# Taking one of the 16 DMA engines out of one late store: 120 partitions and 8 in place of 128

## The chip, the core and the metric

The kernel runs on one core of a Trainium2 chip. Times are microseconds of device time; a time quoted for a kernel is the median of its runs. "Span" is the length of the one profiled execution, and positions in it are counted from its start.

SBUF and PSUM are the memories that the kernel's tiles are allocated in; a tile here has 128 partitions. A *packet* is one row of the trace's DMA table: a piece of a transfer, moved by one DMA engine. A *completion* is one increment of a transfer's semaphore by one DMA engine; the store of a group shows 16 of them in the kernel before. SP is the engine whose instructions issue the transfers.

## The reference

```python
# x: (8, 16, 256, 512) float32, weight: (8, 16, 512, 384) float32
def reference(x, weight):
    return np.matmul(x, weight).astype(np.float32)
```

128 independent products of 256x512 by 512x384. The kernel reads 168 MB and writes 50 MB.

## The kernel before

The kernel takes four products at a time as a "group", 32 groups in all. For each it loads 2 MB of x and twice 1.5 MB of weights, casts both to bf16, transposes x on TensorE, multiplies, copies PSUM to an output tile and stores it. All transfers are issued from one queue (SP). SP loads four groups ahead.

```python
    G = 4; R = G * M // P; T = R // 2; NG = B // G      # R = 8 rows a partition, T = 4, NG = 32
    XS, WS, OS = 2, 2 * G // D, 4                       # buffers of x, weights, output
    LAG = 4
    ...
    out_sb = sbuf("out_sb", [P, R, N], fp32, OS)        # 128 partitions of 8 x 384 x 4 = 12288 B
    ...
    def store(e, t, U, s, pieces=1):
        n = t * U + s
        dram = o_rows[bass.ds(n * (G * M), G * M)].rearrange("(p r) n -> p r n", r=R)
        for q in range(pieces):
            rows = slice(q * R // pieces, (q + 1) * R // pieces)
            e.wait_ge(o_copied, n * T + ((q + 1) * T // pieces + BIAS))
            e.dma_start(out=dram[:, rows], in_=out_sb[s % OS][:, rows]).then_inc(
                o_out[s % OS], 16
            )
    ...
    def on_sync(e):
        U = OS
        for n in range(LAG):
            load(e, 0, NG, n)
        rounds = (NG - LAG) // U
        with e.Fori(0, rounds) as t:
            for s in range(U):
                load(e, t, U, LAG + s)
                store(e, t, U, s)
        for n in range(rounds * U, NG):                 # groups 28 to 31: stores alone are left
            if n + LAG < NG:
                load(e, 0, NG, n + LAG)
            store(e, 0, NG, n, T if n == NG - 1 else 1) # the last group in four pieces
        for s in range(OS):
            e.wait_ge(o_out[s], 16 + 16 * (NG // OS + (T - 1 if s == (NG - 1) % OS else 0)))
```

Of the kernel before, what the change touches and what calls it, by code (L numbers as in the profile page):

```python
# [12 lines left out]
def kernel(  # L13
# [7 lines left out]
    P = 128  # L21

    b1, b2, M, K = x.shape
# [6 lines left out]
    o_rows = out.rearrange("b1 b2 m n -> (b1 b2 m) n")  # L30
# [9 lines left out]
    G = 4  # L40
    C = P // G
    R = G * M // P
    T = R // 2
# [3 lines left out]
    NG = B // G  # L47

    XS, WS, OS = 2, 2 * G // D, 4
    BS, TS, WBS = 1, 2, 2 * G  # L50
    PT, PO = 4, 2

    LAG = 4

    ctx.enter_context(tc.tile_critical(no_gpsimd_drain=True))  # L55

    def sbuf(name, shape, dtype, n):
        return [
            ctx.enter_context(nc.sbuf_tensor(f"{name}{s}", shape, dtype)) for s in range(n)
        ]  # L60
# [6 lines left out]
    def sems(name, n):  # L67
        return [tc.alloc_semaphore(f"{name}{s}") for s in range(n)]
# [9 lines left out]
    out_sb = sbuf("out_sb", [P, R, N], fp32, OS)  # L78
# [6 lines left out]
    id_done, x_cast, w_cast, t_made, t_copied, p_made, o_copied = (  # L85
        sems(name, 1)[0]
        for name in (
            "id_done", "x_cast", "w_cast", "t_made", "t_copied", "p_made", "o_copied"
        )
    )  # L90
    x_in, w_in, o_out = sems("x_in", XS), sems("w_in", WS), sems("o_out", OS)


    BIAS = 8


    def load(e, t, U, s):
        n = t * U + s
        if not isinstance(n, int) or n >= XS:
            e.wait_ge(x_cast, n + (1 - XS))  # L100
        e.dma_start(  # L101
            x_sb[s % XS][:],
            x_rows[bass.ds(n * (G * M), G * M)].rearrange("(p r) k -> p r k", r=R),
        ).then_inc(x_in[s % XS], 16)
        for d in range(G // D):
            slot = (s * (G // D) + d) % WS
            if not isinstance(n, int) or n >= 2:
                e.wait_ge(w_cast, n * (G * S) + ((d + 1) * D * S - 2 * G * S))  # L108
            e.dma_start(  # L109
                w_sb[slot][:],  # L110
                w_rows[bass.ds(n * (G * K) + d * (D * K), D * K)].rearrange(
                    "(p k) n -> p k n", k=S * KO
                ),
            ).then_inc(w_in[slot], 16)
# [6 lines that stand above are left out]
            e.wait_ge(o_copied, n * T + ((q + 1) * T // pieces + BIAS))  # L121
            e.dma_start(out=dram[:, rows], in_=out_sb[s % OS][:, rows]).then_inc(
                o_out[s % OS], 16
            )

    def cast_x(e, t, U, s):
# [80 lines left out]
# [9 lines that stand above are left out]
        for n in range(rounds * U, NG):  # L216
            if n + LAG < NG:
                load(e, 0, NG, n + LAG)
            store(e, 0, NG, n, T if n == NG - 1 else 1)
        for s in range(OS):  # L220
            e.wait_ge(o_out[s], 16 + 16 * (NG // OS + (T - 1 if s == (NG - 1) % OS else 0)))

    def on_vector(e):
        U = 2
# [34 lines left out]

    on_gpsimd(nc.gpsimd)  # L260
    on_sync(nc.sync)
    on_vector(nc.vector)
    on_tensor(nc.tensor)
# [31 lines left out]
```

## Time and profile before

| | before |
|---|---|
| time | 519.69 us (519.62 to 519.71) |
| span of the profiled run | 517.8 us |
| last copy of output ends | 510.80 us |
| last DMA packet ends | 515.97 us |
| last completion arrives | 516.38 us |
| DMA rate in the middle | about 430 GB/s |

The page's lines for this, and what is read from them, are in the prediction below. The trace also dates each packet (start, duration, bytes) and each increment of a semaphore, one for each engine that takes part in a transfer. It does not number the engines.

### The profile page before, as it was taken

The numbers are of one execution on the slowest core, as the hardware profiler recorded it, in microseconds if no ns is written. First come the engines' busy times: TensorE is split into PE (matmuls) and PEld (weight loads), VectorE is DVE, ScalarE is ACT, GpSimd is POOL, SyncE is SP. The second block draws the span as 40 slices with busy tenths as digits, with TensorE's granted clock in tenths as the row PEclk, the third lists the DMA queues.
The fourth block names the chain that finished last, engine by engine and source line by source line (L and its number), as shares of the span: only waits on it lengthen the run. The fifth ranks groups of instructions, "written<-read, shape, count | busy, mean of one in ns | idle before, by whom it ended". The sixth has DMA issues, their size and how long they took to land.

```text
span 517.8 us, 11229 instructions
## 1 busy us (share of the span) xinstructions
PE 314.3 (61%) x4608; PEld 198.2 (38%) x4608; DVE 323.9 (63%) x384; ACT 212.9 (41%) x193; POOL 0.7 (0%) x6
## 2 busy tenths in 40 slices
PE   0588674576655676555766557665566655676653
PEld 0455443343433443333434334343344333443432
DVE  0788867655577555775556765557755577555670
ACT  3156462454324553245533345523455233553332
POOL 0000000000000000000000000000000000000000
PEclk9988896787868886787878678866877686777867
DMA  8999999999999999999999999999999999999995
GB/s 332 433 423 428 425 431 429 429 431 424 428 431 430 428 427 429 429 429 430 431 424 431 429 433 426 426 431 427 432 429 428 427 430 428 432 430 426 428 430 233
DMA packets 18869, 218.18 MB, mean 421 GB/s; under 512 B 2096, under 2 KB 2096, under 8 KB 2608
## 3 DMA queue, kind: packets, MB, share of 16 engines
q1 hardware_dynamic: 18864, 218.11, 99.3%
q8 instruction: 3, 0.05, 0.0%
q14 instruction: 2, 0.02, 0.0%
HBM read 167.77 MB, written 50.33 MB: 421 GB/s over the span
## 4 chain that ended last, share of the span: by engine, by line
DMA 81%; DVE 13%; issue 2%; PE 2%; ACT 1%; SPq 0%; DVEq 0%; ACTq 0%
DMA w_sb<-in_weight_dram 81%; DVE w_bf L149 12%; PE po L182 2%; ACT x_bf L131 0%; DVE x_t L155 0%; SPq L109 0%; ACT out_sb L196 0%; SPq L101 0%; DVEq L144 0%; DVEq L226 0%; SPq L108 0%; ACTq L195 0%; SPq L290 0%; SPq L55 0%
## 5 line engine op out<-in xcount | busy, mean ns | idle before, releaser
L149 DVE CAST w_bf<-w_sb 64x1536 bf16<-64x1536 f32 x256 | 244.5, 955 | 179.1 <-DMA w_sb<-in_weight_dram 172.1
L182 PE MATMUL po<-w_bf,x_t 128*32 128x384 bf16 x4096 | 231.4, 400 | 121.4 <-DVE x_t L155 121.4
L196 ACT COPY out_sb<-po 128x768 f32<-128x768 f32 x128 | 99.4, 803 | 289.3 <-PE po L182 289.3
L182 PEld LDWEIGHTS po<-w_bf,x_t 128*32 128x32 bf16 x4096 | 124.8, 116 | 225.3 <-DVE x_t L155 131.1
L168 PE MATMUL pt<-identity,x_bf 128*128 128x128 f32 x512 | 82.8, 325 | 74.3 <-ACT x_bf L131 74.3
L131 ACT CAST x_bf<-x_sb 128x2048 bf16<-128x2048 f32 x64 | 118.5, 1901 | 7.3 <-DMA x_sb<-in_x_dram 7.3
L168 PEld LDWEIGHTS pt<-identity,x_bf 128*128 128x128 f32 x512 | 73.3, 213 | 86.1 <-issue 86.1
L155 DVE COPY x_t<-pt 128x1024 bf16<-128x1024 bf16 x128 | 79.4, 683 | 1.0
L131 ACT ACT_TABLE_LOAD x1 | 1.3, 1283 | 1.3 <-PEq L232 1.3
masks.py:199 POOL TENSOR_SCALAR_AFFINE_SELECT identity<-identity 128x128 f32<-128x128 f32 x1 | 0.3, 294 | 0.2 <-POOL identity L202 0.2
L202 POOL MEMSET identity<- 128x128 f32 x1 | 0.2, 205 | 0.5 <-SPq L55 0.5
L279 POOL MEMSET const-bfloat16-1.0<- 128x1 bf16 x1 | 0.1, 102 | 0.0
L279 POOL MEMSET const-uint8-127<- 128x1 uint8 x1 | 0.1, 102 | 0.0
L279 POOL MEMSET const-float32-0.0<- 128x1 f32 x1 | 0.1, 99 | 0.2 <-issue 0.2
L279 POOL MEMSET const-float32-1.0<- 128x1 f32 x1 | 0.1, 99 | 0.0
## 6 DMA issues: line engine op xcount, KB each, us to landing
w_sb<-in_weight_dram SPq DMA_DIRECT2D x64, 1536.0 KB, 27.5
x_sb<-in_x_dram SPq DMA_DIRECT2D x32, 2048.0 KB, 25.8
out_dram<-out_sb SPq DMA_DIRECT2D x31, 1536.0 KB, 30.6
out_dram<-out_sb SPq DMA_DIRECT2D x4, 384.0 KB, 4.0
```

The costliest lines, as they stand in the source:

```text
L131: ins = e.copy(out=x_bf[s % BS][:, :, h], in_=x_sb[s % XS][:].rearrange("p r (q s c) -> p r s q c", s=S, c=KO)[:, :, h],)
L149: e.tensor_copy(out=w_bf[(s * G + d * D + a) % WBS][h * HP : (h + 1) * HP], in_=w_sb[slot][a * HP : (a + 1) * HP, h * KO : (h + 1) * KO, : ...
L155: e.tensor_copy(out=x_t[s % TS][:, 2 * q : 2 * q + 2], in_=pt[(s * T + q) % PT][:].bitcast(bf16),).then_inc(t_copied, 1)
L168: ins = e.transpose(pt[(s * T + q) % PT][:, rr, h, :], words[:, 2 * q + rr, h :: KO // 2], identity[:],)
L182: ins = e.matmul(po[(s * T + q) % PO][mine, rr, :N], x_t[s % TS][:, 2 * q + rr, ko // 2, mine, ko % 2], w_bf[(s * G + i) % WBS][:, ko, :], ...
L196: e.copy(out=out_sb[s % OS][:, 2 * q : 2 * q + 2, :], in_=po[(s * T + q) % PO][:, :, :N],).then_inc(o_copied, 1)
L202: e.memset(identity[:], 0.0).then_inc(id_done, 1)
L279: nc = _bacc.Bacc("TRN2", target_bir_lowering=False, num_devices=1)
```

## The change

Its intent: one of the 16 DMA engines, meant to be the last, gets no part of the store of group 28, so that it has less queued ahead of the end. The store is cut into partitions 0 to 119 and partitions 120 to 127. The recorded texts call the engine that is to be left out engine 15; that is a name, since no trace numbers the engines.

```diff
+    SKIP, SKIPPING = 120, NG - OS
...
+    def store_skipping(e, n):
+
+        dram = o_rows[n * (G * M) : (n + 1) * (G * M)].rearrange("(p r) n -> p r n", r=R)
+        e.wait_ge(o_copied, n * T + T + BIAS)
+        for parts in (slice(0, SKIP), slice(SKIP, P)):
+            e.dma_start(out=dram[parts], in_=out_sb[n % OS][parts]).then_inc(
+                o_out[n % OS], 16
+            )
...
-            store(e, 0, NG, n, T if n == NG - 1 else 1)
+            if n == SKIPPING:
+                store_skipping(e, n)
+            else:
+                store(e, 0, NG, n, T if n == NG - 1 else 1)
         for s in range(OS):
-            e.wait_ge(o_out[s], 16 + 16 * (NG // OS + (T - 1 if s == (NG - 1) % OS else 0)))
+            more = {(NG - 1) % OS: T - 1, SKIPPING % OS: 1}.get(s, 0)
+            e.wait_ge(o_out[s], 16 + 16 * (NG // OS + more))
```

## The prediction

> **What bounds the kernel now.** I read the page from the top. Part 2 says which resource is full, part 4 says what the end waited for.
>
> ```profile
> DMA  8999999999999999999999999999999999999995
> GB/s 332 433 423 428 425 431 429 429 431 424 428 431 430 428 427 429 429 429 430 431 424 431 429 433 426 426 431 427 432 429 428 427 430 428 432 430 426 428 430 233
> ...
> q1 hardware_dynamic: 18864, 218.11, 99.3%
> ...
> DMA 81%; DVE 13%; issue 2%; PE 2%; ACT 1%; SPq 0%; DVEq 0%; ACTq 0%
> ```
>
> The 16 DMA engines are busy from the second slice to the last but one and move about 430 GB/s; no compute engine passes 63% of the span. So the transfers set the pace. The chain of part 4 agrees (81% of it is weight loads), but it follows instructions and stops at the last copy into the output buffer. In order of time its end is:
>
> ```profile
> 502.32 7.66 PE po L182 x66
> 510.00 0.80 ACT out_sb L196
> ```
>
> The last piece of output is thus ready at 510.80 us and the span ends at 517.8 us. Those 7 us belong to the stores. The timeline of the DMA queue shows when the last ones were issued, five groups of 1536 KB, the last in four pieces (eight issues):
>
> ```profile
> 470.50 40.66 SPq L122 DMA_DIRECT2D out_dram<-out_sb  x8
> ```
>
> The table of stretches and the DMA view of 512 to 517 us (40 slices of 0.125 us) show how they drain:
>
> ```profile
> 505.00:510.00 5.00, 4.95 (x100) 2.60 (x92) 0.00 (x0) 2.43 (x3) 0.00 (x0) 0.81 0.94 390
> 510.00:512.00 2.00, 0.00 (x0) 0.00 (x0) 0.00 (x0) 0.80 (x1) 0.00 (x0) 1.00 0.79 315
> 512.00:514.00 2.00, 0.00 (x0) 0.00 (x0) 0.00 (x0) 0.00 (x0) 0.00 (x0) 0.94 0.42 167
> 514.00:516.00 2.00, 0.00 (x0) 0.00 (x0) 0.00 (x0) 0.00 (x0) 0.00 (x0) 0.50 0.06 25
> ...
> DMA  9999932321000000000000000010000000000000
> GB/s 393 418 418 393 393 123 98 123 98 74 25 25 25 25 25 25 25 25 25 25 25 25 25 25 25 25 49 25 25 25 25 0 0 0 0 0 0 0 0 0
> ```
>
> Full rate until about 512.6, then 98 to 123 GB/s for half a microsecond, then 25 GB/s until 515.9. One packet of 3072 B in each slice of 0.125 us is 25 GB/s, and a sixteenth of 430 is 27: for the last 2.7 us **one DMA engine works alone**, and 0.06 of 16 engines is one.
>
> That it is one engine that fell behind can be followed in the completions. Every transfer raises its semaphore sixteen times, once for each engine, and the trace dates each. For the stores of some groups, in us, the median of the sixteen and the last one:
>
> ```
> group   median   last    behind
>  4      132.1    133.6     1.5
> 16      322.8    325.3     2.5
> 24      450.0    453.1     3.1
> 28      501.2    504.8     3.6
> 30      508.4    512.7     4.3
> ```
>
> Three others sit some 1.5 us behind all along; three 16 KB instruction fetches of about 1 us each at 6, 35 and 43 us fit that. One falls back steadily. The last group's pieces end, in packets, at about 512.6 us on twelve engines, at 513.2 to 513.3 on the three, and at 515.97 on the slow one; the completions arrive about 0.4 us later, the last at 516.38.
>
> [...] 128 partitions take 16 engines with 8 partitions each (the trace agrees: 8 packets of 12288 B for each completion)[...]. [...] the slow engine's store packets follow each other without a gap to the end. So work left out earlier in its queue moves all later work forward.
>
> **The change part by part.**
> - Removed from engine 15: 8 packets of 12288 B. A packet mostly took 460 to 475 ns, on the slow engine up to 535. Between the slow engine's completions of groups 27 and 28 lie 504.75 - 500.97 = 3.78 us, so about 3.8 us goes.
> - [...]
> - Added on SP: one more issue, 0.36 us, at about 471 us. SP then waits for group 29's copies, done near 481, so it is off the path.
> - Loads: all are issued before this store [...]. The weights land at the same time, the compute ends at the same 510.80 us.
>
> Now the end. If engine 15 is the slow one, its last packet would be at 515.97 - 3.8 = 512.2 us. But the last piece's data is issued after 510.80 us, and engines without backlog end it at about 512.6, so the slow engine joins those. The end passes to the three engines that are 1.5 us behind: last completion at 513.65. That is 516.38 - 513.65 = **2.73 us** earlier. [...] After the last completion, 1.4 us to the span's end stays. In time: 519.69 - 2.73 = 516.96, or 519.69 - 2.26 = 517.43. I cannot tell which from this trace[...], so I lean to 517.3.
>
> **The rivals.**
> - *The slow engine is not the fifteenth.* [...] For it: the trace has no engine numbers. Against it: the change singles out the last engine, and the 3.8 us that it takes away is nearly the amount by which one engine is behind when this store runs (3.6 us). I give this one in ten.
> - *The stores are hidden or the compute sets the end.* Then freeing an engine brings nothing below what compute allows. It speaks for this that the last issue is at 510.8 us and twelve engines end already at 513.0. It is a floor: at most 516.38 - 513.0 = 3.4 us can be had, 516.3.
> - *The 120-partition transfer is dealt out otherwise*, on fewer engines. If all the first part ran on 8 engines, each would carry 15 packets in place of 8 and the end would move out by about 3 us less what slack there is: 521 to 523. [...] Under one in twenty.
> - *The whole kernel speeds up by the slow engine's share.* No: nothing before 471 us changes, and the loads are already queued.
>
> **Range and chances.** The two branches give 516.96 and 517.43; the runs before lie within 0.1 us. A little less gain than worked out is possible if the freed engine or the piece issues queue otherwise, so the range is 516.7 to 518.1 us. Two per cent is 10.4 us: no branch gets there. Faster by over 2%: 0.01, within: 0.98, slower: 0.01.
>
> **What would show it.** In the profile after: the stores' issues are one more, one of 1440 KB and one of 96 KB; the stretch of 25 GB/s at the end is gone or shorter than half a microsecond; the last copy still ends near 510.8 us; the last completion is at 513.6 to 514.1 us; after the changed store no engine is over 2 us behind. If the 25 GB/s stretch is still 2.7 us long, the wrong engine was spared; if the last copy moved, something upstream changed, which I do not expect.

Passages are cut from this text, and with them terms of its sum: which engines get the small transfer, what that adds (one packet of 12288 B and one completion each, 0.47 us, the author's estimate from packets of 460 ns), and how the others were to absorb it. No trace on hand then showed how a transfer of 120 or of 8 partitions is shared out. The sum came to 2.73 us less, 516.96, if none of the three engines that end next carries an added packet, and to 2.26 us less, 517.43, if one does; the forecast was 517.3. The first rival put 519.7 if the slow engine has no part in the small transfer, and 520.2 if it has. That work left out earlier moves later work forward was measured afterwards: with no store of group 28 the kernel takes 516.73 us in place of 519.88 (experiment 10).

## The result, and the profile after

The changed kernel takes 524.24 us (523.35 to 524.89, four runs; the profiled one is the slowest of them) against 519.70 us for the kernel before in the same rounds (519.62 to 519.85). The ratio is 1.0086, 95% interval 1.0068 to 1.0103: slower by nearly one per cent, where a gain of half a per cent was predicted. (A ratio here is the mean time of one kernel's fast runs over that of the other's fast runs of the same rounds, so not quite the ratio of the medians.)

The page of the profile after, its parts 2, 3, 4 and 6:

```profile
GB/s 335 430 424 428 423 429 429 430 429 426 429 428 428 431 426 430 424 430 431 428 430 425 430 431 428 431 425 429 431 430 430 427 427 430 429 429 432 424 361 135
...
q1 hardware_dynamic: 18871, 218.11, 98.6%
...
DMA 80%; DVE 12%; issue 2%; PE 2%; ACT 1%; SPq 0%; DVEq 0%; ACTq 0%
...
out_dram<-out_sb SPq DMA_DIRECT2D x30, 1536.0 KB, 30.6
out_dram<-out_sb SPq DMA_DIRECT2D x4, 384.0 KB, 4.7
out_dram<-out_sb SPq DMA_DIRECT2D x1, 1440.0 KB
out_dram<-out_sb SPq DMA_DIRECT2D x1, 96.0 KB
```

The two parts of the store are there (1440 and 96 KB), the bytes moved are the same, and 38 of 40 slices look as before. The difference is in the last two slices: 361 and 135 GB/s where before 430 and 233 stood.

The timeline of the SP queue after (start, duration, line, count) shows the issues where they were expected:

```profile
471.01 0.36 SPq L124 DMA_DIRECT2D out_dram<-out_sb  x1
471.58 0.78 SPq L133 DMA_DIRECT2D out_dram<-out_sb  x2
482.06 29.80 SPq L124 DMA_DIRECT2D out_dram<-out_sb  x6
```

The chain in order of time still ends in the last copy:

```profile
510.37 0.80 ACT out_sb L207
```

That copy ends at 511.17 us, 0.4 later than before; the last weights landed 0.5 us later too (494.2 against 493.7), before anything unusual is seen in the transfers. So compute is not what was lost. The tables of stretches (columns: stretch, its length, busy time of PE, weight loads, DVE, ACT and POOL, granted clock, DMA share, GB/s), first of the kernel before, up to where the prediction's rows begin, then of the kernel after:

```profile
495.00:500.00 5.00, 2.73 (x16) 2.33 (x16) 4.84 (x6) 1.58 (x3) 0.00 (x0) 0.67 1.01 430
500.00:505.00 5.00, 2.67 (x36) 1.37 (x40) 4.00 (x6) 0.00 (x0) 0.00 (x0) 0.50 1.02 433
```

```profile
495.00:500.00 5.00, 2.88 (x16) 2.48 (x16) 4.84 (x6) 2.02 (x3) 0.00 (x0) 0.69 1.02 406
500.00:505.00 5.00, 2.18 (x28) 1.08 (x32) 4.47 (x7) 0.00 (x0) 0.00 (x0) 0.50 0.99 337
505.00:510.00 5.00, 5.00 (x104) 2.84 (x96) 0.00 (x0) 2.40 (x3) 0.00 (x0) 0.78 0.92 363
...
514.00:516.00 2.00, 0.00 (x0) 0.00 (x0) 0.00 (x0) 0.00 (x0) 0.00 (x0) 0.50 0.29 120
516.00:518.00 2.00, 0.00 (x0) 0.00 (x0) 0.00 (x0) 0.00 (x0) 0.00 (x0) 0.50 0.14 58
518.00:520.00 2.00, 0.00 (x0) 0.00 (x0) 0.00 (x0) 0.00 (x0) 0.00 (x0) 0.50 0.06 26
520.00:522.00 2.00, 0.00 (x0) 0.00 (x0) 0.00 (x0) 0.00 (x0) 0.00 (x0) 0.50 0.04 15
```

**The pair of columns to read is the last two.** From 500 to 505 us the engines are as busy as before (0.99) and move 337 GB/s in place of 433. Busy engines that move less: their packets take longer. And the stretch of one engine alone is still there, at 518 to 521 us.

The packets say it directly. Those of 12288 B that start after 494 us, by duration:

```
                 up to 600 ns   over 600 ns   longest
before                497             0         541
after                 447            54        1600
```

The first long one starts at 497.27 us, when the first engines come to group 28. The completions of the engine that was last before, and is last again, can be followed, since it ends every group last (in us; in brackets, the time since the line above):

```
                      before                     after
group 27 done         500.97                     502.60
group 28, 8 packets   504.75   (3.78)            510.09   (7.49)
one packet more         -                        510.61   (0.52)
group 29              508.78   (4.03)            514.32   (3.71)
group 30              512.69   (3.91)            517.98   (3.66)
last piece            516.38                     521.68
```

Two things are plain. The slow engine was **not spared**: it has its 8 packets of group 28, done at 510.09 us, and one of the added packets too, done at 510.61. And its 8 packets took 7.5 us in place of 3.8. The packets that lie end to end between these two completions took 562, 940, 946, 967, 684, 932, 956 and 1442 ns; in the kernel before, one of 12288 B takes 460 to 541 ns near the end. The spared engine can be seen as well: one completion of group 29 arrives at 501.34 us, the next one at 504.67. An engine that was not late ran 3.3 us ahead of all others, and nothing waited for it.

The sum over the slow engine: 1.63 us by group 27, 3.71 on group 28, 0.52 for the packet, less 0.57 regained on groups 29 and 30, gives 5.3 us, which is the 521.68 - 516.38 of the end and the 523.1 - 517.8 of the spans. Not all of the 1.63 us is the change's: 0.5 us was there at group 26 (485.53 against 485.04), before any part of group 28 moved, and the profiled runs of this document spread from 485.0 to 485.8 there. From group 26 to group 27 the last completion takes 17.07 us in place of 15.93, so the change accounts for 1.1 us, and for 4.8 of the 5.3 us in all. The median loss is 4.5 us.

### The profile page after: what moved, and what is told of

Its sections match the earlier page's. It is cut to its first block, busy times and chain, and to the rows that moved or that the text cites. A ratio compares the mean times of both kernels' runs of the same rounds, so it can differ in the third digit from the quotient of the medians.

```text
span 523.1 us, 11230 instructions
## 1 busy us (share of the span) xinstructions
PE 314.9 (60%) x4608; PEld 197.7 (38%) x4608; DVE 324.0 (62%) x384; ACT 212.7 (41%) x193; POOL 0.7 (0%) x6
## 4 chain that ended last, share of the span: by engine, by line
DMA 80%; DVE 12%; issue 2%; PE 2%; ACT 1%; SPq 0%; DVEq 0%; ACTq 0%
DMA w_sb<-in_weight_dram 80%; DVE w_bf L160 12%; PE po L193 2%; ACT x_bf L142 0%; DVE x_t L166 0%; SPq L111 0%; ACT out_sb L207 0%; SPq L103 0%; DVEq L155 0%; DVEq L241 0%; SPq L110 0%; ACTq L206 0%; SPq L305 0%; SPq L57 0%
```

## The experiments

**Theory A.** The slow engine is not the one that was left out, and in addition a store that is cut by partitions makes packets that move at the same time slow each other, depending on which partitions a transfer takes. **Rival B.** The 8-partition transfer is what costs. **Rival C.** Something about 15 engines, or about the rows in HBM, makes packets long.

What the packets of theory A would meet on was an assumption that no trace here shows. The ranges for theory A stand, as estimates from packets of 460 ns. In all experiments but the second the result is wrong on purpose. The diffs are against the changed kernel unless one names another; where the number of transfers changes, so does the number of completions waited for at the end, which is left out below. Each run has a profile, and times are of three rounds beside the kernel before.

### 1. Only the 120-partition transfer

```diff
-        for parts in (slice(0, SKIP), slice(SKIP, P)):
+        for parts in (slice(0, SKIP),):          # and one completion less at the end
```

> Only the 120-partition transfer of group 28; its last 8 partitions are never written (wrong result on purpose). Theory A ([...] the slow engine is not the one spared): still slow, about 523 to 524 us, with packets of 12288 B at 900 ns and more from 497 us on. Rival B (the 8-partition transfer, 8 engines on few partitions, is the whole cost, the slow engine is not spared): 519.5 to 520.0. My blind step (the slow engine is spared, only the small transfer spoils it): about 517.

Measured: 523.9 us (522.42 to 524.14), ratio 1.0075 (1.0058 to 1.0091); 42 packets of 12288 B over 600 ns. Rival B falls: without the small transfer, nearly the whole loss is there (4.3 us of 4.5). The stretches of this run:

```profile
500.00:505.00 5.00, 2.52 (x32) 1.29 (x36) 4.15 (x6) 0.00 (x0) 0.00 (x0) 0.64 0.99 359
...
518.00:520.00 2.00, 0.00 (x0) 0.00 (x0) 0.00 (x0) 0.00 (x0) 0.00 (x0) 0.50 0.06 25
```

Again 0.99 busy at a reduced rate, and one engine alone at 518 us.

### 2. Two halves of 64 partitions, nobody spared

```diff
-        for parts in (slice(0, SKIP), slice(SKIP, P)):
+        for parts in (slice(0, 64), slice(64, P)):
```

> Group 28 as partitions 0 to 63 and 64 to 127; [...] no engine spared, no engine has more packets, only one completion more. Theory A: [...] most packets of the group take about 920 ns in place of 460, 3.7 us more an engine: 522.5 to 525. Rival B or a cost that is special to 15 engines: 519.5 to 520.

Measured: 523.4 us (522.92 to 523.82), ratio 1.0073 (1.0056 to 1.0090), result correct; 52 packets over 600 ns.

```profile
500.00:505.00 5.00, 2.42 (x32) 1.24 (x36) 4.26 (x6) 0.00 (x0) 0.00 (x0) 0.65 0.96 320
```

The rate falls most of all runs here, to 320 GB/s, though the semaphore counts 32 updates for this group, 16 for each half, which reads as no engine left out. The full store ahead of the halves ends late too: 17.29 us from group 26 to group 27, in place of 15.93. So the number 15 is not the cause, nor is the sparing of an engine. What 64 + 64 and 120 have in common is that the store is cut by partitions. That a store is cut in pieces is not enough: the last group's four pieces, cut by rows and not by partitions, have packets of 3072 B of at most 127 ns in the kernel before.

### 3. The full transfer, and 8 partitions more

```diff
+        e.dma_start(out=dram, in_=out_sb[n % OS][:]).then_inc(o_out[n % OS], 16)
+        other = o_rows[0 : G * M].rearrange("(p r) n -> p r n", r=R)   # rows of group 0: wrong there
-        for parts in (slice(0, SKIP), slice(SKIP, P)):
-            e.dma_start(out=dram[parts], in_=out_sb[n % OS][parts]).then_inc(
+        for parts in (slice(SKIP, P),):
+            e.dma_start(out=other[parts], in_=out_sb[n % OS][parts]).then_inc(
```

> The full 128-partition transfer of group 28, then partitions 120 to 127 once more into rows of group 0 (wrong result there on purpose). Theory A: [...] the slow engine, if it is among them, ends 0.5 to 2 us later: 520.2 to 521.7; if it is not, 519.7. Rival B: 523 to 524.5, as the change.

"Them" are the engines that the small transfer gives a packet to.

Measured: 520.29 us against 519.61, ratio 1.0013 (0.9996 to 1.0030). Three packets over 600 ns. The small transfer's whole price is 0.7 us, near the limit of what the interval tells from none.

### 4. to 8. Which engine is the slow one

The probe: four extra transfers of k partitions after the full store of group 28. An engine that takes part in each gets four packets more, some 1.9 us (an estimate, 4 x 0.47). The end moves only if the slow engine is among those that get them. The engine numbers here are names given by this probe and no trace shows them: number j is what transfers of j + 1 partitions load and those of j do not, so that k partitions load "0 to k - 1". That a larger k loads what a smaller one does is shown for the slow engine alone (below, k = 5 to 8). The partitions are 4 apart.

```diff
-        for parts in (slice(SKIP, P),):                        # of experiment 3
+        for parts in (slice(j, 4 * k, 4) for j in range(4)):   # k = 8, 7, 4, 5, 6
```

> Which engine is the slow one: the full transfer of group 28, then four transfers of 8 partitions 4 apart (wrong rows of group 0 on purpose)[...]. Adds 4 x 0.47 = 1.9 us [...]. If the slow engine is among 0 to 7: 521.6. If it is among 8 to 15: 519.7, since the three late engines at 513.65 + 1.9 stay ahead of 516.4.

> As the run with four extra transfers of 8 partitions 4 apart, but of 7 partitions[...]. If the slow engine is number 7: 519.7, nothing added at the end. If it is among 0 to 6: 521.6 to 522.1.

> The same with 4 partitions[...]. If the slow engine is among 0 to 3: 521.6 to 522.1. If it is among 4 to 7: 519.7.

> Four extra transfers of 5 partitions[...]. By the runs with 7 and 4 the slow engine is number 4, 5 or 6. If it is 4: 521.5 to 522. If 5 or 6: 519.7 to 520.

> Four extra transfers of 6 partitions[...]. If the slow engine is 4 or 5: 521.5 to 522. If it is 6: 519.7 to 520.

| k | engines loaded, as named | measured | kernel before beside it | ratio (95%) |
|---|---|---|---|---|
| 8 | 0 to 7 | 522.06 | 519.61 | 1.0044 (1.0028 to 1.0061) |
| 7 | 0 to 6 | 521.53 | 519.88 | 1.0035 (1.0018 to 1.0052) |
| 6 | 0 to 5 | 521.59 | 519.83 | 1.0032 (1.0016 to 1.0049) |
| 5 | 0 to 4 | 521.79 | 519.83 | 1.0037 (1.0020 to 1.0054) |
| 4 | 0 to 3 | 519.83 | 519.88 | 0.9999 (0.9982 to 1.0016) |

Between k = 4 and k = 5 lie 2 us: **transfers of 5 partitions load the slow engine, and transfers of 4 do not**. By the count of this probe it is number 4. (The runs with 7, 6, 5 and 4 were on one chip, the one with 8 on another, where it shows no more than that transfers of 8 partitions load the slow engine.) The DMA views of the end (512 to 523 us, slices of 0.275 us), first k = 4, then k = 8:

```profile
GB/s 380 145 369 380 424 246 78 34 22 22 34 22 22 34 22 22 34 0 0 0 0 0 0 0 0 0 0 0 0 0 0 0 0 0 0 0 0 0 0 0
```

```profile
GB/s 380 324 290 235 257 156 156 89 34 11 34 22 22 34 22 22 34 22 22 34 22 22 34 0 0 0 0 0 0 0 0 0 0 0 0 0 0 0 0 0
```

The tail of 22 to 34 GB/s is one engine alone; with k = 8 it ends six slices later, 1.7 us. And none of these extra transfers, partitions 4 apart, made a packet of over 600 ns: not one in any of the five runs.

### 9. The same 32 partitions, adjacent

```diff
-        for parts in (slice(j, 32, 4) for j in range(4)):          # experiment 4, k = 8
+        for parts in (slice(8 * j, 8 * j + 8) for j in range(4)):
```

> As the run with four extra transfers of 8 partitions 4 apart (522.06), the same partitions 0 to 31 in all, the same bytes to the same rows[...]; but each transfer takes 8 adjacent partitions[...]. [...] some packets of 12288 B at 900 to 1900 ns after 500 us, and 522.5 to 526. If it is something about the number of engines, the bytes or the rows of HBM: 521.5 to 522.3 and no long packets.

The first range is that of theory A.

Measured: 522.14 us (522.03 to 522.19), ratio 1.0043. The expectation of the packets held, that of the time did not. Of 12288 B packets over 600 ns there are 11, up to 1402 ns; with the partitions 4 apart there was none. The number of transfers, the bytes and the HBM rows as a whole are the same in both, and so is the count of packets under 512 B, the completions' own (4 B each), from 496 to 508 us (82); which partitions share a transfer differs. So it is not which HBM rows are written as a whole, nor by that count how many engines take part. Which engine writes which of these rows may have changed along with the partitions, so the HBM side is not out by this run alone; experiments 11 and 12 say more. The time is that of experiment 4 all the same. The trace dates the long packets between 500.9 and 507.2 us. Nine of the eleven are not the slow engine's. Its four extra packets, found end to end between its completions, took 492, 496, 632 and 1008 ns, against 491, 502, 515 and 534 ns in experiment 4. That is 0.6 us more, which is about the spread of the runs of experiment 4 (521.51 to 522.23 us).

### 10. No store of group 28 at all

```diff
-        for parts in (slice(0, SKIP), slice(SKIP, P)):
-            e.dma_start(...).then_inc(o_out[n % OS], 16)           # nothing is issued
```

> Group 28 isn't stored at all (wrong result on purpose): every engine has 8 packets less ahead of the end. My blind reading of the end: the slow engine would be done 3.8 us earlier but the last piece is issued after the last copy, so the end is at 516.3 to 516.6: the most that any sparing of an engine in this group could bring. If the end were set by something else than the slow engine's queue: 519.7, or 519.7 less 3.8 = 515.9 if no floor is there.

Measured: 516.73 us (516.06 to 517.28), ratio 0.9940 (0.9923 to 0.9957), 0.1 us above the range expected. The DMA view of the end, 512 to 523 us:

```profile
GB/s 380 436 391 90 0 0 0 0 0 0 0 0 0 0 0 0 0 0 0 0 0 0 0 0 0 0 0 0 0 0 0 0 0 0 0 0 0 0 0 0
```

The lone engine's tail is gone; all end together with the last piece. So the reading of the end was right, and about 3 us is the most that any sparing of an engine in this group could win.

### 11. and 12. Packets on chosen partitions, none added to the slow engine

```diff
-        for parts in (slice(j, 32, 4) for j in range(4)):           # experiment 4
+        for parts in (slice(16, 20), slice(48, 52)):                # 11; 12: (24, 28) and (56, 60)
```

The author took partitions 16 to 19 and 48 to 51 for such as would meet the slow engine's own, and 24 to 27 and 56 to 59 for such as would meet another engine's; what that choice rested on is shown by no trace. In the first, the range up to 523.5 is that of theory A, at most 8 x 0.46 = 3.7 us more (an estimate, from packets of 460 ns). In the second the times could not tell; theory A expected long packets, its opposite none.

> After the full transfer of group 28, two extra transfers of 4 adjacent partitions, 16 to 19 and 48 to 51[...]. Engine 4 itself gets no packet. [...] 522 to 523.5, with long packets. If only an engine's own queue counts: 519.7 to 520.2.

> The same with partitions 24 to 27 and 56 to 59[...]: in either case 519.7 to 520.3[...].

Measured: 520.86 (ratio 1.0020, 1.0004 to 1.0037) and 520.66 us (1.0017, 1.0000 to 1.0034). The first lies between what the two sides expected, the second above what either did, and the times alone do not tell the two choices apart. The packets do. Each run has 11 or 12 packets over 600 ns, the longest 3579 and 3739 ns, eight times the usual 460. Seven and eight of them stand alone before a completion, as the extra packets do. The other four follow each other in both runs on a single engine, with no completion between: 609, 904, 939 and 715 ns in the first, 874, 913, 922 and 899 in the second. All other packets of the full stores stay under 600 ns. So the extra packets slow one single engine out of those that run full stores at the same time. The author would expect a shortage on HBM in general to slow more than one, and takes rival C to be out in that form; no run shows that by itself. One form of it was not tested: the extra rows belong to partition numbers that the stores of groups 28 and 29 write too, exactly 28 or 29 groups later on HBM. Where the packets meet, no trace shows.

Whose packets these are can be followed in the completions of the slow engine:

```
                 before     16-19, 48-51       24-27, 56-59
group 27 done    500.97     501.59             501.06
group 28         504.75     506.54  (4.95)     504.83  (3.77)
group 29         508.78     510.53             508.84
group 30         512.69     514.34             512.71
its last piece   516.38     518.05             516.43
span's last      516.38     518.05             517.37
```

In the first run the eight packets between the slow engine's completions of groups 27 and 28 are 465, 460, 471, 609, 904, 939, 715 and 475 ns: the four long ones are among them. It took 4.95 us in place of 3.78, 1.2 us more, and the time rose by 1.1 us. (Another 0.6 us of the column was there at group 26, within the spread given above.) In the second run it is not delayed (3.77 us). Another engine ends last there: its last completion of group 28, at 506.28 us, follows an extra packet of 2515 ns, and it stays last to 517.37. So the slow engine **was delayed without a packet of its own added**, by packets on partitions 16 to 19 and 48 to 51, and not by those on 24 to 27 and 56 to 59. These two runs were on the chip of experiment 4.

## Why the prediction was wrong

- **What bounds the end: right.** The store queues do, and the floor below them is the last piece: with no store of group 28 at all the time is 516.73, where the prediction's floor said 516.3.
- **How many engines take part, 15 and 8: right, as far as the updates tell.** Issues of 1440 and 96 KB. Of group 28 the semaphore shows 25 updates where a full store shows 16. Two of them come at 472.14 and 472.53 us, right after the two issues; the other 23, from 500.81 to 510.61 us, fit 15 engines for the 120 packets, 8 a completion as in the kernel before, and 8 for the 8.
- **"If engine 15 is the slow one": this step failed.** It carried the whole gain and was given nine chances in ten. In the changed kernel's trace the slow engine has its 8 packets and one more, and by experiments 4 to 8 transfers of 5 partitions reach it (521.79 us against 519.83 with 4). The 3.8 us were taken from an engine that was not late. The prediction itself noted that the trace has no engine numbers, then leaned on the change's wording and on 3.8 being close to 3.6 us; neither is evidence of which engine it was.
- **The added packet, 0.47 us for an engine that gets one (above): nearly right.** The extra packet cost the slow engine 0.52 us in the trace, and experiment 3 gives 0.7 us in the time. With this term alone, the first rival's 520.2 would have come true, and did in experiment 3 (520.29).
- **The duration of a packet: the term that was missing.** The sum took 460 to 475 ns for any packet of 12288 B, whoever carries it. That holds for the transfers of 128 partitions in the kernel before, where no packet after 494 us takes over 541 ns (the slow engine's take 484 to 541 near the end, a little more than the 535 that was read). In the 120-partition transfer the slow engine's 8 packets took 7.49 us in place of 3.78, and it lost 1.6 us on group 27 beforehand, of which 1.1 us are the change's, while engines ahead of it were already reading group 28. Experiments 1 and 2 show that this comes from cutting the 128 partitions and not from the small transfer or the spared engine. Experiments 9, 11 and 12 show that it counts which partitions a transfer takes: 8 adjacent ones made 11 packets over 600 ns where 8 that are 4 apart made none, and 16 to 19 and 48 to 51 slowed the slow engine where 24 to 27 and 56 to 59 did not.
- **The third rival** (dealt out otherwise, 521 to 523, under one in twenty) had the direction and nearly the size, but for a cause, fewer engines, that is not what happened.
- **Compute and loads: as predicted**, within the 0.4 to 0.5 us named above.

What stays open: what the packets meet on; how the 120 partitions are shared out among the engines; why the slow engine is slow; and whether sparing it would win anything. Of the extra transfers of 4 to 8 partitions, 4 apart, only those of 4 left it out (519.83 us), and sparing it was not tried. No correct version tested beats the kernel before.

## What to carry to other kernels

When a profile shows one DMA engine finishing alone, find out which one before taking work from it: a few extra transfers of k partitions, k stepped down, show in a handful of runs which of them reach it. Do not count a transfer of fewer than 128 partitions by its bytes alone, but try which partitions it takes: here a store cut as 120 + 8 or 64 + 64 made 54 and 52 packets over 600 ns, where 460 is usual, and extra packets on partitions 16 to 19 and 48 to 51 made four of the slow engine's packets take 609 to 939 ns, while extra transfers of partitions 4 apart made no long packet. A sign of it, in these runs, was a DMA share that stays near 1.0 while the GB/s fall (0.99 at 337 GB/s, 0.96 at 320).
